# A decoder layer in split fp32r: the order of the twelve products of a half step

## The chip, the cores and the metric

The kernel runs on one core of one Trainium2 chip. The metric is the device time of one execution in microseconds (us); a lower time is better. Three runs of the kernel before gave a median of 2371.65 us (2369.32 to 2371.7).

## The reference, cut to what matters

One decoder layer is computed for 256 tokens of 2048 channels, in fp32. Two gated feed-forward nets lie around a mixer that adds a retention branch and a windowed attention branch:

```python
x = x + 0.5 * mod[:, 2] * swiglu(modulate(rms_norm(x, norm_ffn1)), w_ffn1_gu, w_ffn1_down)
h = modulate(rms_norm(x, norm_mix))
x = x + mod[:, 5] * token_mixing(h, w_in, w_ret_branch, w_swa_branch, w_out, sinks)
x = x + 0.5 * mod[:, 8] * swiglu(modulate(rms_norm(x, norm_ffn2)), w_ffn2_gu, w_ffn2_down)
return rms_norm(x, norm_final)
```

Nearly all of the arithmetic is in products of the 256 token rows with big fp32 weights (2048 x 11264, 5632 x 2048, 2048 x 13312 and three of 2048 x 2048). `mod` comes from a condition vector `c` and a weight of 2048 x 18432, as sums over products rather than as a matrix product on the tensor engine.

## The kernel before, in words

**Splitting.** A number is split into a high part (rounded to fp32r) and a low part (the difference), and a product of two numbers is made of three: high by high, low activation by high weight, and high activation by low weight. `split` (L365 to L373) makes the two parts of a weight tile: ScalarE casts `wh` (L369), VectorE subtracts `wl` (L371). Activations are split the same way, either once into a held pair (`Held`, tiles `hh` and `hl`) or when they are used (`Whole.pair`, cast L404 and subtraction L405, tile `a`).

**Tiling.** A weight block is 512 of the contracted channels by 512 columns (1 MB, one DMA, `load`, L346, four buffers `raw`). A half of it, 256 channels by 512 columns, is one half step: one call of `split` and one call of `products`. The 256 tokens are two tiles of 128 (t = 0 and 1), each with a PSUM bank of its own that accumulates over the half steps. `wh` and `wl` have three buffers each (pool `wsp`), and the accumulating banks four (`acc`). A half step has two blocks of 128 channels (j), two token tiles (t) and three products, so twelve matmuls of 128 x 128 by 128 x 512. The stationary operand is a 128 x 128 piece of the activation, the moving one a 128 x 512 piece of the weight.

**Order in `products` (L349 to L363).** The loops run over j, then over t, and inside that come the three products of one j and one t: L356 high by high, L357 low activation, L359 low weight. All three add into the same bank. The last matmul is put into the list `newest`, which other code uses to place its own matmuls behind it (`issue_after(newest[-1])`).

**Who sets the order on the engines.** For most of the kernel the order of the program is a priority only: a scheduler with a timeline model goes through the instructions, and each engine is given the first one in program order whose inputs are ready in that model. So what an engine runs can differ from the program's order. Only the sync engine's queue (the weight loads) is always in written order. In the stages marked `manual_schedule(engines=ORDERED)`, which are the start and the ends of the three down products, PE, DVE and ACT too run in written order. There `last` calls `products` for one t at a time, and a written list (`ORDER`) interleaves the parts of it with a norm.

**What else uses the engines.** `gemm` and `gemm_part` walk the half steps; after each `products` call `tick` adds some passes of the conditioning sums (VectorE, L219). The softmax of the windowed attention and the retention run beside the input projection (between about 860 and 1210 us of the span). Results leave the banks through VectorE or ScalarE (L637, L702, L1158 and others).

Of the kernel before, what the change touches and what calls it, by code (L numbers as in the profile page):

```python
# [17 lines left out]
P = 128  # L18
# [59 lines left out]
def layer_kernel(  # L78
# [22 lines left out]
    nc = tc.nc  # L101
# [246 lines left out]

    def products(banks, ah, al, wh, wl, starts, ends, halves=range(NT)):  # L349
        n = ah.shape[1]  # L350
        for j in range(n):
            first, last = starts and j == 0, ends and j == n - 1
            for t in halves:
                ts = slice(t * P, (t + 1) * P)
                ps = banks[t]
                nc.tensor.matmul(ps, ah[:, j, ts], wh[:, j, :], start=first, stop=False)  # L356
                nc.tensor.matmul(ps, al[:, j, ts], wh[:, j, :], start=False, stop=False)  # L357
                newest.append(
                    nc.tensor.matmul(  # L359
                        ps, ah[:, j, ts], wl[:, j, :], start=False, stop=last  # L360
                    ).ins
                )
                del newest[:-1]  # L363

    def split(pool, tag, src, n, hi_engine="act"):  # L365
        k = src.shape[1]
# [8 lines left out]
    cast, low, newest = [], [], []  # L375
# [48 lines left out]
    def gemm_part(act, w, col0s, banks, kb, KT, ahead=None, close=None):  # L424

        pairs = [act.pair(kb * 2 + h) for h in range(2)]
        for i, c0 in enumerate(col0s):
            raw = None if ahead else load(w, kb, c0)
            for h in range(2):
                if ahead:  # L430
                    wh, wl = ahead[h]
                else:
                    wh, wl = split(wsp, "w", raw[:, 2 * h : 2 * h + 2, :], CH)
                ah, al = pairs[h]
                ends = kb * KB + 2 * h + 2 == KT or (i == close and h == 1)
                products(banks[i], ah, al, wh, wl, kb + h == 0, ends)
                tick()
            turn_step()

    def gemm(act, w, col0s, KT=KD, ahead=None):  # L440
        banks = [[acc_bank() for _ in range(NT)] for _ in col0s]
        for kb in range(KT // KB):
            gemm_part(act, w, col0s, banks, kb, KT, None if kb else ahead)
            step()
        return banks
# [285 lines left out]
    def down_product(act, w, gate, KT, spare, before, after, parted=False):  # L731
# [16 lines left out]
        with tc.manual_schedule(engines=ORDERED):  # L748
# [16 lines left out]
            for kb in (a - 2, a - 1, a, b):  # L765
                wt = weight(w, kb, c0s[0])
                pairs[kb] = []
                for h in range(2):
                    pairs[kb].append(act.pair(kb * 2 + h, place(kb, h)))
                    products(  # L770
                        banks[0], *pairs[kb][h], *wt(h), kb + h == 0, kb == b and h == 1
                    )
                n = {a - 2: a - 2, a - 1: a, a: b, b: a - 1}[kb]
                wt = weight(
                    w, n, c0s[1], spare if n == a - 2 else None if n < a else home_views()
                )
                late[n] = [(n, h, wt(h)) for h in range(2)]
            steps = [step for kb in (a - 2, a, a - 1, b) for step in late[kb]]

            def last(t, which, to=None, cs=slice(0, CH)):  # L780
                to = banks[1] if to is None else to
                for kb, h, (wh, wl) in which:
                    starts = kb == a - 2 and h == 0 if parted else kb + h == 0
                    products(
                        to, *pairs[kb][h], wh[:, :, cs], wl[:, :, cs],
                        starts, kb == b and h == 1, [t],
                    )
# [260 lines left out]
    banks, moved = {}, set()  # L1048
# [118 lines left out]
    for g, ks in enumerate(groups):  # L1167
# [7 lines left out]
        for i, n in enumerate(order):  # L1175
# [5 lines left out]
            last = len(order) - 2  # L1181
# [94 lines left out]
    halves = [slice(i * HD, (i + 1) * HD) for i in range(2)]  # L1276
# [227 lines left out]
    def gates(p):  # L1504

        sg = slot().rearrange("p (g i t n) -> p g i t n", g=2, i=2, t=NT)
        for g, off in ((0, O_GR), (1, O_GS)):
            for i in range(2):
                b = in_chunk(off + (2 * p + i) * CH)
                for t in range(NT):  # L1510
                    nc.scalar.activation(sg[:, g, i, t, :], b[t], AF.Sigmoid)
        return sg

    first = gates(0)
# [17 lines left out]
    for p in range(2):  # L1532
        sg = first if p == 0 else gates(p)
        c0s = [(2 * p + i) * CH for i in range(2)]
        for g, a, w in ((1, a_swa, w_swa_branch), (0, a_ret, w_ret_branch)):
            assert g == 1 or not turns
            banks = gemm(a, w[0], c0s)
# [149 lines left out]
```

## Time and profile before

| what | value |
|---|---|
| three runs, median | 2371.65 us (2369.32 to 2371.7) |
| profiled execution, first to last instruction (span) | 2366.2 us |
| PE (matmul) busy | 2343.0 us, 99% |
| PEld (weight load) busy | 1920.2 us, 81% |
| DVE busy | 1703.8 us, 72% |
| ACT busy | 1312.3 us, 55% |
| HBM | 254 GB/s over the span |

The profile gives no time for the profiled execution other than its span, which is 5.45 us below the median of the runs. PE is the matmul queue, PEld the loads of the stationary operand, DVE the vector engine, ACT the scalar engine, SP the engine that issues the weight loads. "L359" is line 359 of the kernel. A row "out<-in" names the tile written and the tiles read. Idle time stands before an instruction, with the engine or DMA that ended it. A matmul's recorded end is modelled, and records of consecutive matmuls overlap, so the distance between two starts is what shows the rate.

### The profile page before, as it was taken

What the parts mean: (1) busy time and instruction counts of PE and PEld (TensorE: products, weight loads), DVE (VectorE), ACT (ScalarE), POOL (GpSimd) and SP (SyncE); (2) the same over time, 40 slices, a digit from 0 to 9 for tenths busy, and PEclk for the clock granted to TensorE, in tenths of its full rate; (3) what the DMA queues carried; (4) which work ended last, traced back from release to release, by engine and by line L of the source; (5) the groups of instructions that cost most, each with busy time, mean ns of one, the idle gap of its engine ahead of it and who ended that gap; (6) DMA issues with size and microseconds to landing.
All of it is one profiled execution on the core that took longest, in us unless ns stands there. A gap on an engine that the chain in (4) does not pass through costs nothing.

```text
span 2366.2 us, 28355 instructions
## 1 busy us (share of the span) xinstructions
PE 2343.0 (99%) x10479; PEld 1920.2 (81%) x10479; DVE 1703.8 (72%) x2628; ACT 1312.3 (55%) x1780; POOL 9.2 (0%) x21
## 2 busy tenths in 40 slices
PE   8999999999999999999999999999999999999998
PEld 5888888888788887778888888888888888888887
DVE  7887799778877768976777776677555555555656
ACT  6544456455546568775556564466455455455544
POOL 0000000000000000000000000000000000000000
PEclk9999999999999999999999999999999999999999
DMA  9977789998866889876778787764777777666553
GB/s 385 362 289 268 273 294 356 347 346 334 315 251 231 282 274 238 252 222 244 271 275 292 300 297 282 289 208 179 246 237 257 247 240 262 239 214 203 193 196 125
DMA packets 186316, 627.87 MB, mean 265 GB/s; under 512 B 108801, under 2 KB 109185, under 8 KB 115649
## 3 DMA queue, kind: packets, MB, share of 16 engines
q1 hardware_dynamic: 183682, 615.05, 74.8%
q0 software_dynamic: 1600, 9.83, 1.0%
q8 instruction: 82, 1.34, 0.2%
q10 hardware_dynamic: 896, 1.19, 0.1%
q14 instruction: 56, 0.46, 0.1%
HBM read 597.16 MB, written 4.22 MB: 254 GB/s over the span
## 4 chain that ended last, share of the span: by engine, by line
PE 55%; DVE 1%; issue 0%; ACT 0%; DVEq 0%
PE pa L359 18%; PE pa L356 18%; PE pa L357 18%; DVE wl L371 0%; PE ps L1372 0%; PE pd L1457 0%; PE pd L1471 0%; PE pd L1470 0%; PE pd L1472 0%; PE ps L888 0%; DVE spare L480 0%; DVE soft L1359 0%; PE ps L359 0%; PE ps L357 0%; PE ps L356 0%
## 5 line engine op out<-in xcount | busy, mean ns | idle before, releaser
L369 ACT CAST wh<-raw 128x1024 fp32r<-128x1024 f32 x792 | 831.7, 1053 | 915.3 <-PE pa L357 881.4
L371 DVE TENSOR_TENSOR wl<-raw,wh 128x1024 fp32r<-128x1024 f32 x792 | 961.3, 1222 | 519.4 <-ACT wh L369 516.3
L356 PE MATMUL pa<-wh,hh 128*128 128x512 f32 x2184 | 854.0, 391 | 1.7 <-ACT wh L369 1.7
L357 PE MATMUL pa<-wh,hl 128*128 128x512 f32 x2184 | 850.4, 389 | 0.0
L359 PE MATMUL pa<-wl,hh 128*128 128x512 f32 x2184 | 773.3, 391 | 1.9 <-DVE wl L371 1.8
L356 PEld LDWEIGHTS pa<-wh,hh 128*128 128x128 f32 x2184 | 409.9, 188 | 90.3 <-ACT wh L369 2.8
L359 PEld LDWEIGHTS pa<-wl,hh 128*128 128x128 f32 x2184 | 408.3, 188 | 91.1 <-DVE wl L371 5.5
L357 PEld LDWEIGHTS pa<-wh,hl 128*128 128x128 f32 x2184 | 410.1, 188 | 84.7 <-issue 0.2
L357 PE MATMUL pa<-wh,a 128*128 128x512 f32 x912 | 353.4, 389 | 0.3 <-DVE a L405 0.3
L356 PE MATMUL pa<-wh,a 128*128 128x512 f32 x912 | 337.6, 389 | 1.8 <-DVE t L637 1.8
L359 PE MATMUL pa<-wl,a 128*128 128x512 f32 x912 | 335.8, 389 | 0.4 <-DVE wl L371 0.4
L219 DVE CUSTOM_DVE_ANT_0 slot<-slot,cact 128x512 f32<-128x512 f32 (+2 forms) x272 | 209.4, 819 | 12.8 <-DMA slot<-in_w_ada_dram 12.7
L356 PEld LDWEIGHTS pa<-wh,a 128*128 128x128 f32 x912 | 171.0, 188 | 37.7 <-DVE t L637 2.2
L357 PEld LDWEIGHTS pa<-wh,a 128*128 128x128 f32 x912 | 171.1, 188 | 37.2 <-DVE a L405 1.9
L359 PEld LDWEIGHTS pa<-wl,a 128*128 128x128 f32 x912 | 171.1, 188 | 36.1 <-DVE wl L371 0.8
L545 ACT COPY slot<-back 128x512 uint16<-128x512 uint16 x140 | 93.3, 765 | 0.0
L219 DVE CUSTOM_DVE_ANT_0 rows_x<-rows_x,cact 128x512 f32<-128x512 f32 x124 | 78.7, 687 | 11.3 <-DMA rows_x<-in_w_ada_dram 10.9
L219 DVE CUSTOM_DVE_ANT_0 raw<-raw,cact 128x512 f32<-128x512 f32 (+1 forms) x108 | 70.8, 706 | 18.3 <-DMA raw<-in_w_ada_dram 18.0
L405 DVE TENSOR_TENSOR a<-slot,a 128x512 fp32r<-128x512 f32 x114 | 77.8, 684 | 0.3 <-ACT a L404 0.3
L529 ACT COPY flat<-t 128x512 uint16<-128x512 uint16 x128 | 72.7, 617 | 3.0 <-DVE t L1445 2.5
L404 ACT CAST a<-slot 128x512 fp32r<-128x512 f32 x114 | 70.3, 618 | 0.1
L219 DVE DVE_READ_ACCUMULATOR2_ANT sums<- 128x1 f32 x504 | 41.1, 82 | 0.0
(252 smaller groups left out, 1246.7 us busy)
## 6 DMA issues: line engine op xcount, KB each, us to landing
raw<-in_w_ffn_gu_dram SPq DMA_DIRECT2D x160, 1024.0 KB, 5.1
raw<-in_w_in_dram SPq DMA_DIRECT2D x104, 1024.0 KB, 5.8
raw<-in_w_ffn_down_dram SPq DMA_DIRECT2D x88, 1024.0 KB, 4.9
slot<-in_w_ada_dram SPq DMA_DIRECT2D x83, 1024.0 KB, 7.0
rows_x<-in_w_ada_dram SPq DMA_DIRECT2D x31, 1024.0 KB, 7.1
raw<-in_w_ada_dram SPq DMA_DIRECT2D x26, 1024.0 KB, 5.7
raw<-in_w_swa_branch_dram SPq DMA_DIRECT2D x16, 1024.0 KB, 6.4
raw<-in_w_ret_branch_dram SPq DMA_DIRECT2D x16, 1024.0 KB, 5.5
```

Of the source, the lines that this page charges most:

```text
L219: nc.vector.tensor_tensor_reduce(out=w[:, at], in0=w[:, at], in1=cact[:, at], scale=1.0, scalar=0.0, op0=ALU.mult, op1=ALU.add, accum_out= ...
L356: nc.tensor.matmul(ps, ah[:, j, ts], wh[:, j, :], start=first, stop=False)
L357: nc.tensor.matmul(ps, al[:, j, ts], wh[:, j, :], start=False, stop=False)
L359: nc.tensor.matmul(ps, ah[:, j, ts], wl[:, j, :], start=False, stop=last).ins
L369: cast.append(nc.scalar.copy(hi, src).ins)
L371: low.append(nc.vector.tensor_sub(lo, src, hi.bitcast(F32)).ins)
L404: nc.scalar.copy(hi, v)
L405: nc.vector.tensor_sub(lo, v, hi.bitcast(F32))
L529: nc.scalar.copy(planes[:, i, :], words(src)[:, :, i])
L545: nc.scalar.copy(into[:, :, :, i], held["turned"][:, i])
```

## The change

The three products become the outer loop. First come the four high by high products of the half step (j = 0 with both t, j = 1 with both t), then the four with the activation's low part, then the four with the weight's low part. The number of matmuls, their operands and their sizes are the same. The first matmul of the first row starts the accumulation of its bank, and the last row ends it. `newest` holds the last matmul of the call.

```diff
     def products(banks, ah, al, wh, wl, starts, ends, halves=range(NT)):
         n = ah.shape[1]
-        for j in range(n):
-            first, last = starts and j == 0, ends and j == n - 1
-            for t in halves:
-                ts = slice(t * P, (t + 1) * P)
-                ps = banks[t]
-                nc.tensor.matmul(ps, ah[:, j, ts], wh[:, j, :], start=first, stop=False)
-                nc.tensor.matmul(ps, al[:, j, ts], wh[:, j, :], start=False, stop=False)
-                newest.append(
-                    nc.tensor.matmul(
-                        ps, ah[:, j, ts], wl[:, j, :], start=False, stop=last
-                    ).ins
-                )
-                del newest[:-1]
+        parts = ((ah, wh), (al, wh), (ah, wl))
+        for i, (act, weights) in enumerate(parts):
+            for j in range(n):
+                for t in halves:
+                    product = nc.tensor.matmul(
+                        banks[t],
+                        act[:, j, t * P : (t + 1) * P],
+                        weights[:, j, :],
+                        start=starts and i == 0 and j == 0,
+                        stop=ends and i == 2 and j == n - 1,
+                    )
+        newest.append(product.ins)
+        del newest[:-1]
```

## Prediction, written before the change was run

> **What bounds the kernel now.** I read the page first: which engine fills the span, and the costliest groups.
>
> ```profile
> span 2366.2 us, 28355 instructions
> PE 2343.0 (99%) x10479; PEld 1920.2 (81%) x10479; DVE 1703.8 (72%) x2628; ACT 1312.3 (55%) x1780; POOL 9.2 (0%) x21
> ...
> L369 ACT CAST wh<-raw 128x1024 fp32r<-128x1024 f32 x792 | 831.7, 1053 | 915.3 <-PE pa L357 881.4
> L371 DVE TENSOR_TENSOR wl<-raw,wh 128x1024 fp32r<-128x1024 f32 x792 | 961.3, 1222 | 519.4 <-ACT wh L369 516.3
> L356 PE MATMUL pa<-wh,hh 128*128 128x512 f32 x2184 | 854.0, 391 | 1.7 <-ACT wh L369 1.7
> L357 PE MATMUL pa<-wh,hl 128*128 128x512 f32 x2184 | 850.4, 389 | 0.0
> L359 PE MATMUL pa<-wl,hh 128*128 128x512 f32 x2184 | 773.3, 391 | 1.9 <-DVE wl L371 1.8
> ...
> L357 PE MATMUL pa<-wh,a 128*128 128x512 f32 x912 | 353.4, 389 | 0.3 <-DVE a L405 0.3
> ```
>
> PE fills 99% of the span. Each of the three lines runs 2184 + 912 = 3096 times in the two big groups alone, so 9288 products, or 774 half steps of twelve. The last columns say how little PE waits. ScalarE, by contrast, sat idle for 881.4 us because it waited for the last product that reads an old `wh`: the splits are made ahead, as far as the three buffers allow.
>
> Second, the busy time by window, for the rate of a stretch with nothing but products, and the granted clock by core:
>
> ```profile
> 1800.00:1900.00 100.00, 100.00 (x443) 82.81 (x442) 57.69 (x76) 49.76 (x57) 0.00 (x0) 1.00 0.72 244
> core 0: 2366.2 us, clock 0.999
> ```
>
> The first count is that of PE: 100 us hold about 441 whole products (443 touch the window), so 0.227 us each; the clock is fully granted. Nothing in the change alters this rate unless the order itself does, which the timeline of PE can show, since the scheduler already strays from the written order:
>
> ```profile
> 1700.19 0.39 PE L357 MATMUL pa<-wh,hl 128*128 128x512 f32 x1
> 1700.41 0.39 PE L356 MATMUL pa<-wh,hh 128*128 128x512 f32 x1
> 1700.64 0.39 PE L357 MATMUL pa<-wh,hl 128*128 128x512 f32 x1
> 1700.87 0.62 PE L359 MATMUL pa<-wl,hh 128*128 128x512 f32 x2
> 1701.32 0.39 PE L356 MATMUL pa<-wh,hh 128*128 128x512 f32 x1
> ```
>
> Here the two token tiles' high and low-activation products run first and the two low-weight products follow as a pair: in this group the first low-weight product is already the fifth of its half step, not the third. The pair takes 0.62 us, which is 0.39 + 0.23, and the next starts 0.45 us after the pair began: two products on two banks, with the same moving tile, at 0.225 us each. Steps within one bank (L356 to L357) take 0.22 to 0.23 us too. So the order as such is free in this trace.
>
> That leaves the waits of the two PE queues, third:
>
> ```profile
> PE pa L359 <- DVE wl L371: 2.5, 6, 0.9
> PE pa L356 <- DVE t L637: 1.8, 1, 1.8
> PE pa L356 <- ACT wh L369: 1.7, 2, 1.2
> PE pa L357 <- DVE a L405: 0.3, 1, 0.3
> ...
> PEld pa L359 <- DVE wl L371: 7.6, 15, 1.3
> PEld pa L357 <- DVE a L405: 1.9, 4, 0.7
> ```
>
> The waits for a low part of a weight (`wl`) and of an activation (`a`) are all that the new order can relieve directly. The rest of the span that isn't products is the start, the small matmuls of softmax and retention and the norm at the end, which the change leaves alone.
>
> **What a wait costs.** The columns are total us, times, longest. A PE row counts only idle time behind a matmul's modelled end, 0.39 us after its start, whereas the next could start after 0.227; so 0.16 us of each wait is missing. The timeline around some of the waits shows this and a second loss:
>
> ```profile
> 862.97 0.39 PE L357 MATMUL pa<-wh,hl 128*128 128x512 f32 x1
> 863.87 0.73 PE L359 MATMUL pa<-wl,hh 128*128 128x512 f32 x2 [0.51 <-DVE wl L371]
> ...
> 42.90 0.39 PE L357 MATMUL pa<-wh,hl 128*128 128x512 f32 x1
> 43.48 0.73 PE L359 MATMUL pa<-wl,hh 128*128 128x512 f32 x2 [0.19 <-DVE wl L371]
> ...
> 48.15 0.50 PE L356 MATMUL pa<-wh,hh 128*128 128x512 f32 x1 [1.20 <-ACT wh L369]
> ...
> 62.20 0.39 PE L357 MATMUL pa<-wh,hl 128*128 128x512 f32 x1
> 62.76 0.73 PE L359 MATMUL pa<-wl,hh 128*128 128x512 f32 x2 [0.18 <-DVE wl L371]
> ...
> 1042.93 0.39 PE L359 MATMUL pa<-wl,hh 128*128 128x512 f32 x1
> 1044.24 0.74 PE L359 MATMUL pa<-wl,hh 128*128 128x512 f32 x2 [0.92 <-DVE wl L371]
> ```
>
> At 863.87 the start is 0.90 us after the one before it, so 0.67 late; and the pair behind it takes 0.73 instead of 0.62, so 0.11 more, 0.78 in all for an idle time of 0.51. So each wait in a PE row costs its idle time and 0.16 + 0.11 = 0.27 more; a wait that shows only in the load queue is hidden under the modelled end and costs between 0 and 0.27.
>
> **The change part by part.**
>
> Nothing is removed or added: same matmuls, same loads, same DMAs, and SP's and POOL's queues are not passed by anything. Four things move.
>
> First, the low weight's first use. In the written order it is third, in the scheduled one often fifth; it becomes ninth, so 4 to 6 products or 0.91 to 1.36 us later. What the six and the nine hidden `wl` waits cost now: 2.5 + 6 x 0.27 = 4.1 us, and 0 to 9 x 0.27 = 2.4 more, so 4.1 to 6.5.
>
> Second, the low activation's first use goes from second or third to fifth, 0.45 to 0.68 us later. What those waits cost now: 0.3 + 0.27 = 0.57, and 0 to 3 x 0.27 = 0.8 more, so 0.6 to 1.4. Together 4.7 to 7.9; I take the middle, 6.3 us, as what both sorts of wait cost now.
>
> Third, `wh` is read last by the eighth product instead of the eleventh, so its buffer is free 0.68 us earlier. The cast (1.05 us) and the subtraction (1.22 us) behind it begin that much sooner, though the subtraction still needs the buffer of `wl`, which comes free with the twelfth as before. The cast alone takes 4.6 products, so it ends about when the twelfth does: nothing new waits there. This adds up to 0.68 us of slack for each split and could relieve the two `wh` waits (1.7 + 2 x 0.27 = 2.2 us); I count none of it, since the wait at 48.15 stands in a crowded stretch, and keep 2.2 for the range.
>
> Fourth, the second token tile's bank is needed by the second product instead of the fourth, 0.45 us sooner. That matters only where a bank is just being emptied. There is one such wait in the trace, for L637 (1.8 us), and I leave it as it is; the cost is 0 to 0.45.
>
> What of the 6.3 goes? The new slack of 0.91 us or more covers a delay of 0.67 at 863.87 or 0.35 at 43.48. It does not cover all of 1044.24: that start is 1.31 us after the one before, so 1.08 late, and 0.17 with its 0.11 would stay: 0.3 is kept. In the first 70 us a removed wait is likely to be found again: the two quoted there cost 0.46 and 0.44 (0.35 + 0.11 and 0.33 + 0.11), and at 48.15 PE waits 1.2 us for a cast, which a PE that comes earlier only waits longer for. Of these 0.9 I keep half, 0.45. Lastly, the scheduler draws up a new plan with the new order, and the new plan will have late tiles of its own. No row shows how many. The bounds are: none, or as many as now (6.3 over 19 waits, and the gain gone). With more slack everywhere I take three of the mean size 0.33, about 0.9 us. Sum: -6.3 + 0.3 + 0.45 + 0.9 = -4.65.
>
> So the profiled execution's 2366.2 us would become 2361.5. That span is 5.45 us under the median of the runs, and I take the same difference from the median: 2371.65 - 4.65 = 2367.0 us, 0.196% less. About 0.2%, or 4.7 us, is what a measurement of this kernel can tell from no change; the forecast lies on that line.
>
> **The rivals.**
>
> *The waits go somewhere else (no change that can be measured).* ScalarE and VectorE then bound those stretches and not the order: the 1.2 us wait for a cast five us behind 43.48 speaks for it, against it stands that DVE is 72% busy and that its splits wait for PE most of the time. If half of the 6.3 comes back, as waits for `wh` or in the new plan, 3.2 us are left: 2368.5.
>
> *Every wait goes (clearly faster).* All 7.9 of the upper bound and the 2.2 of the `wh` waits: 10.1 us, so 2361.6. Against it: the crowded start.
>
> *A change of bank at each product costs time (slower).* Before, the written order changes bank four times in twelve products, after it twelve times; 774 half steps make 8 x 774 = 6192 more changes. At p ns each that is 6.2 x p us. It cancels the gain at 0.75 ns, and at 1.5 ns the kernel is slower by 9.3 - 4.65 = 4.65, at 2376.3. Against it speaks the pair at 1700.87, which changes bank at an unaltered rate, within the rows' hundredths. For it: those rows show only two products in a row that change bank, so a long alternation is not shown.
> [...]
>
> *The new plan is worse (slower).* The softmax and retention stretch has its small matmuls placed behind the newest product; a plan that puts bursts on DVE before the splits would bring more waits like that at 1044.24 (1.08 + 0.11 = 1.2 us). Four of them (4.8 us) use up the forecast gain, and from there it is slower; eight of them, 9.6 us, give 2376.6. Against it: every split has slack added and none removed.
>
> That the change doesn't do what it says is possible in part: the scheduler already runs part of the low-weight products late, so for those half steps the new order is nearer to the old one than the diff looks. This is in the sum through the fifth place.
>
> **How the numbers follow.** My forecast with all waits but a few gone: 0.44 for a gain around 4 to 6 us. Half of it given back: 0.33. Every wait gone: 0.10. Bank changes: 0.05. A worse plan: 0.08. Of the forecast, which lies on the line, three quarters count as faster (0.33), with the 0.10 of the third case 0.43; the rest and the half-gain case are within 0.2%, 0.11 + 0.33 = 0.44; the two slow cases make 0.05 + 0.08 = 0.13. The likeliest time is 2367.0. The range takes in the every-wait-gone case (2361.6, and 1 us for the scatter of the runs below it) and most of the two slower cases (2376.3 and 2376.6): 2360.5 to 2376.5.
>
> **What would show it.** In the changed profile the timeline of PE should read four high, four low-activation and four low-weight products, 0.227 us apart. The waits of PE and its load queue for `wl` should fall from 2.5 and 7.6 us to under 1 and 3, those for `a` to near 0. ScalarE's wait for PE should name the low-activation product as before and stay near 881 us. A window of products only should still hold about 443. I am wrong if that count falls by one or more in a hundred us (banks or clock), if the granted clock falls below 0.995, or if waits for `wh` grow by what those for `wl` lose.

## The result, and the profile after

| | before | after |
|---|---|---|
| median of five runs | 2371.55 us (2369.32 to 2371.7) | 2360.42 us (2359.91 to 2361.44) |
| span of the profiled execution | 2366.2 us | 2359.1 us |

The ratio is 0.996 (95% interval 0.9949 to 0.9971): the new order is faster by 0.3 to 0.5%, 11.1 us between the medians. The forecast was 2367.0, so the direction was right and the gain was more than twice the 4.65 us of the sum; the time lies 0.08 us below the stated range. The kernel before had lower medians in the groups of runs further down, 2368.89 to 2369.87 us over 23 to 27 runs each. Against those the gain would be 8.5 to 9.5 us, but the kernel after was not run in those groups, so 11.1 us, from five runs of each, may be somewhat too much. One run of a kernel further down, the new order with three raw blocks, took 4809 us for a reason that is not known; that kernel's median is 2368.01 us with this run and 2367.72 without it.

The page of the kernel after, its span, its engines, and the groups that answer to those of before (all products stand on line 355 now):

```profile
span 2359.1 us, 28364 instructions
PE 2338.8 (99%) x10479; PEld 1921.2 (81%) x10479; DVE 1697.5 (72%) x2628; ACT 1314.8 (56%) x1779; POOL 9.2 (0%) x21
...
L369 ACT CAST wh<-raw 128x1024 fp32r<-128x1024 f32 x792 | 831.1, 1054 | 883.3 <-PE pa L355 836.7
L371 DVE TENSOR_TENSOR wl<-raw,wh 128x1024 fp32r<-128x1024 f32 x792 | 960.8, 1222 | 478.0 <-ACT wh L369 416.6
L355 PE MATMUL pa<-wh,hh 128*128 128x512 f32 x2184 | 595.5, 392 | 2.2 <-ACT wh L369 1.6
L355 PE MATMUL pa<-wh,hl 128*128 128x512 f32 x2184 | 589.7, 389 | 0.0
L355 PE MATMUL pa<-wl,hh 128*128 128x512 f32 x2184 | 585.2, 390 | 0.4 <-DVE wl L371 0.3
```

The work is the same, instruction for instruction on PE. What fell is idle time before the `wl` products (1.9 to 0.4 us here) and the time for which DVE waited for a cast (516.3 to 416.6 us). The busy us of the PE rows can't be compared with before, since overlapping records of one line are counted once.

The timeline of PE and a window of products only, kernel after:

```profile
1699.74 1.07 PE L355 MATMUL pa<-wh,hh 128*128 128x512 f32 x4
1700.64 1.07 PE L355 MATMUL pa<-wh,hl 128*128 128x512 f32 x4
1701.55 1.07 PE L355 MATMUL pa<-wl,hh 128*128 128x512 f32 x4
1702.46 1.07 PE L355 MATMUL pa<-wh,hh 128*128 128x512 f32 x4
```

```profile
1800.00:1900.00 100.00, 100.00 (x443) 82.81 (x442) 56.96 (x74) 52.46 (x63) 0.00 (x0) 1.00 0.72 237
```

Four of each sort, 0.907 us from row to row, 0.227 each, and 443 matmuls in the window as before. So a change of bank at every product costs nothing that this window shows; its clock reads 1.00 (third from the end), as in the same window of before.

The waits of PE and of its load queue in the kernel after:

```profile
PE pa L355 <- ACT wh L369: 1.6, 3, 1.0
PE pa L355 <- DVE slot L1540: 0.6, 1, 0.6
PE pa L355 <- DVE wl L371: 0.3, 1, 0.3
...
PEld pa L355 <- ACT wh L369: 4.2, 6, 1.4
PEld pa L355 <- DVE wl L371: 1.3, 2, 0.7
PEld pa L355 <- DVE a L405: 0.4, 1, 0.4
```

Waits for `wl` fell from 6 and 15 to 1 and 2, those for `a` from 1 and 4 to 0 and 1. The wait for a bank (L637, 1.8 us) is gone as well; one of 0.6 us for another bank (L1540) is new. Most signs came as forecast. One did not: ScalarE's wait for PE was to stay near 881 us, and it fell to 836.7 (the row of L369 above). That row belongs to the third step of the prediction, the earlier release of the high weight, to which its sum gave nothing. The next question is where 11.1 us can come from when the waits that I could find came to 6.3.

### The profile page after: what moved, and what is told of

Same layout as the page of the kernel before. It is cut to its first block, busy times and chain, and to the rows that moved or that the text cites. A ratio compares the mean times of both kernels' runs of the same rounds, so it can differ in the third digit from the quotient of the medians.

```text
span 2359.1 us, 28364 instructions
## 1 busy us (share of the span) xinstructions
PE 2338.8 (99%) x10479; PEld 1921.2 (81%) x10479; DVE 1697.5 (72%) x2628; ACT 1314.8 (56%) x1779; POOL 9.2 (0%) x21
## 4 chain that ended last, share of the span: by engine, by line
PE 97%; DMA 1%; DVE 1%; ACT 0%; issue 0%; SPq 0%; DVEq 0%; ACTq 0%
PE pa L355 95%; PE ps L1372 0%; DMA slot<-in_w_ada_dram 0%; DMA rows_x<-in_w_ada_dram 0%; PE pd L1288 0%; DVE slot L219 0%; DMA x_sb<-in_x_dram 0%; PE ps L355 0%; PE ps L888 0%; DVE wl L371 0%; PE ps L512 0%; ACT wh L369 0%; DVE rows_x L219 0%; PE ps L1288 0%; PE pd L1470 0%
## 5 line engine op out<-in xcount | busy, mean ns | idle before, releaser
L369 ACT CAST wh<-raw 128x1024 fp32r<-128x1024 f32 x792 | 831.1, 1054 | 883.3 <-PE pa L355 836.7
L371 DVE TENSOR_TENSOR wl<-raw,wh 128x1024 fp32r<-128x1024 f32 x792 | 960.8, 1222 | 478.0 <-ACT wh L369 416.6
L355 PE MATMUL pa<-wh,hh 128*128 128x512 f32 x2184 | 595.5, 392 | 2.2 <-ACT wh L369 1.6
L355 PE MATMUL pa<-wh,hl 128*128 128x512 f32 x2184 | 589.7, 389 | 0.0
L355 PE MATMUL pa<-wl,hh 128*128 128x512 f32 x2184 | 585.2, 390 | 0.4 <-DVE wl L371 0.3
L355 PE MATMUL pa<-wh,a 128*128 128x512 f32 x1824 | 452.4, 389 | 0.0
L355 PE MATMUL pa<-wl,a 128*128 128x512 f32 x912 | 245.2, 389 | 0.0
L1155 DVE TENSOR_TENSOR slot<-slot,pa 128x512 f32<-128x512 f32 x48 | 31.0, 683 | 16.7 <-PE pa L355 16.7
L355 PE MATMUL pa<-wh,home 128*128 128x512 f32 x160 | 39.5, 389 | 0.0
```

The costliest lines, as they stand in the source:

```text
L355: product = nc.tensor.matmul(banks[t], act[:, j, t * P : (t + 1) * P], weights[:, j, :], start=starts and i == 0 and j == 0, stop=ends and ...
L369: cast.append(nc.scalar.copy(hi, src).ins)
L371: low.append(nc.vector.tensor_sub(lo, src, hi.bitcast(F32)).ins)
L1155: nc.vector.tensor_add(p, p, b)
```

## The experiments

The twelve kernels were run in three groups of four, each group on one chip together with runs of the kernel before. A kernel is compared with the median of before in its own group: 2368.89 us for the first four, 2369.63 for the next four, 2369.87 for the last four.

**The kernel before, profiled again.** No edit.

> The kernel before, unchanged, profiled once more. The first profile had a span of 2366.2 us while the runs had a median of 2371.55; the kernel after has 2359.1 and 2360.42, so the gap between the two kernels is 7.1 us by span and 11.1 us by run time. If the first profile of before caught a short execution, this span is about 2369 to 2370 (2371.5 less the 1.8 us that lie outside the span in the run of after) and shows more or longer waits. If the 5.4 us really lie outside the span in this kernel, this span is 2366 again. Ratio to before 1.000.

Measured: 2370.78 us, ratio 1.0004 (0.9995 to 1.0013); the span of this profile is 2370.6. The first part came true, a little above the 2369 to 2370 us expected. In every run 1.7 to 1.9 us lie outside the span, for both kernels, so the first profile of before was an execution of about 2368.0 us, shorter than all five runs beside it. This one, 2372.4 us, is a long one: the spans of the 23 runs of before in this group reach from 2365.0 to 2371.1 us. The waits of the long execution:

```profile
PE pa L359 <- DVE wl L371: 4.5, 8, 1.4
PE pa L356 <- DVE t L637: 1.8, 1, 1.8
PE pa L356 <- ACT wh L369: 1.7, 2, 1.2
...
PEld pa L359 <- DVE wl L371: 11.3, 18, 1.8
```

Waits for `wl` are 11.3 us instead of 7.6 in the load queue. Comparing the starts of the matmuls tells where. The table holds the start of the n-th matmul of the trace, in us from the start of the span, in the kernel after less that in the two executions of before (in the two orders the n-th matmul need not be the same product):

| matmul no. | its start, short execution of before | after less short execution | after less long execution |
|---|---|---|---|
| 200 | 68 us | -0.49 | -0.46 |
| 1400 | 337 us | -0.42 | -0.41 |
| 2000 | 471 us | -0.56 | -4.58 |
| 2300 | 539 us | -0.92 | -4.95 |
| 2800 | 656 us | -4.28 | -9.24 |
| 4600 | 1045 us | -7.19 | -11.26 |
| 6100 | 1379 us | -5.71 | -9.98 |
| last | 2358 us | -7.15 | -11.54 |

The 4 us between 337 and 471 us are there in one execution and not in the other. The timeline of DVE in the long one shows one of their sources:

```profile
464.92 2.36 DVE L371 TENSOR_TENSOR wl<-raw,wh 128x1024 fp32r<-128x1024 f32 x2 [5.62 <-ACT wh L369]
469.56 0.69 DVE L219 CUSTOM_DVE_ANT_0 slot<-slot,cact 128x512 f32<-128x512 f32 x1 [2.27 <-DMA slot<-in_w_ada_dram]
...
472.01 2.36 DVE L371 TENSOR_TENSOR wl<-raw,wh 128x1024 fp32r<-128x1024 f32 x2
```

A conditioning pass waits 2.27 us for its row, and the next two subtractions stand behind it until 472.01; PE then starts a `wl` product 1.74 us after the one before it, at 473.29. In the short execution the pass ahead of the same subtraction did not wait for its row. So how late a row lands differs from one execution to the next, and the old order pays a sum that varies. In the stretch from 640 us, where the wait for the bank stands, a second thing differs. PE in the long execution:

```profile
641.63 0.50 PE L356 MATMUL pa<-wh,a 128*128 128x512 f32 x1 [1.77 <-DVE t L637]
641.97 0.40 PE L357 MATMUL pa<-wh,a 128*128 128x512 f32 x1
642.76 1.22 PE L359 MATMUL pa<-wl,a 128*128 128x512 f32 x2 [0.40 <-DVE wl L371]
643.78 0.63 PE L356 MATMUL pa<-wh,a 128*128 128x512 f32 x1
644.21 0.63 PE L357 MATMUL pa<-wh,a 128*128 128x512 f32 x1
644.63 0.63 PE L359 MATMUL pa<-wl,a 128*128 128x512 f32 x1
...
646.94 0.39 PE L359 MATMUL pa<-wl,a 128*128 128x512 f32 x1
```

```profile
643.40:646.00 2.60, 2.60 (x8) 2.02 (x7) 2.60 (x4) 0.98 (x3) 0.00 (x0) 0.50 0.03 6
646.00:649.00 3.00, 3.00 (x15) 2.46 (x13) 3.00 (x9) 1.96 (x5) 0.00 (x0) 0.98 0.98 350
```

After the same two waits that the short execution had, six products come 0.427 us apart instead of 0.227, and the clock column (third from the end) reads 0.50. That is 1.2 us more for the wait. I had priced a wait at its idle time and 0.27.

**The order taken apart.** Four kernels change only `products`, from the new order. The first keeps the rows and goes bank by bank inside a row:

```diff
-            for j in range(n):
-                for t in halves:
+            for t in halves:
+                for j in range(n):
```

> Rows as in the changed kernel, but inside a row both products of one bank come first and then both of the other, so there are six changes of bank in a half step instead of twelve. Theory of slack (low parts needed later): as the changed kernel, 2360.4, within 1 us. Rival, the bank changes cost time: at p ns each there are some 5000 fewer, so 5 us less per ns; faster than the changed kernel by over 1 us would speak for it. A window of products alone should hold 443 matmuls in 100 us either way by the first theory.

Measured: 2362.71 us, ratio 0.9973 (0.9962 to 0.9984). That is 6.2 us under before, with half of the bank changes. It is not faster than the new order, so the rival of the bank changes falls; it is 2.3 us slower, where 1 us was expected at most, for a reason that was not looked for.

The second puts the low weight's row in the middle:

```diff
-        parts = ((ah, wh), (al, wh), (ah, wl))
+        parts = ((ah, wh), (ah, wl), (al, wh))
```

> Rows in the order high, low weight, low activation: the low weight is first needed by the fifth product, where the scheduled order of before mostly had it, the high weight is read last by the twelfth product (before: eleventh, changed: eighth), and the low activation is first needed by the ninth. Theory of slack for the low weight: most of its waits come back, about 4 to 5 us, so 2365 to 2366 if the second down-product half keeps its 3.4 us and 2369 if not. Rival, the gain is in how the banks are closed (both banks' last products are neighbours, so the vector engine's plan empties both before it turns to other work): nothing but that matters, so 2361 to 2362. Rival, the earlier release of the high weight is what counts: worse than before, above 2371.

Measured: 2369.70 us, ratio 1.0007 (0.9998 to 1.0016). Nothing is left of the gain, though the wait for the bank at L637 is gone in this kernel too. So how the banks are closed is not the cause. The low weight is needed early again here, but the high weight is also held to the end, so two theories are still alive.

The third keeps high and low activation together and moves only the low-weight products:

```diff
...
+        turns = [(p, j, t) for j in range(n) for t in halves for p in (high, low_a)]
+        turns += [(low_w, j, t) for j in range(n) for t in halves]
...
```

> High and low activation stay neighbours as in before, for each block and bank, and only the four low-weight products are moved to the end; so the low weight is first needed by the ninth product, the low activation by the second, and the high weight is read last by the eighth. Theory of slack for the low weight: keeps all but the waits for low activations (four of them, about 1.2 us), so 2361 to 2362. If the rows as a whole (bank changes at each product, low activation later) were what counted, it would be nearer to before: 2365 or more.

Measured: 2360.95 us, ratio 0.9965 (0.9952 to 0.9977). That is 7.9 us under before, and within 0.6 us of the time of the new order, without rows and with the low activation still needed second. Here too the low weight is late and the high weight is free early.

**Late need or early release.** The two are told apart by the next pair. One needs the low weight late and holds the high weight to the last product:

```diff
...
+        turns = rows[0] + rows[1][:-1] + rows[2] + rows[1][-1:]
...
```

> Order of a half step: four high, three low activation, four low weight, and the last low-activation product at the very end. The low weight is first needed by the eighth product (changed kernel: ninth, before: mostly fifth), but the high weight is read last by the twelfth (changed: eighth, before: eleventh). Theory that the later need of the low weight is the cause: near the changed kernel, 6 to 8 us under before. Theory that both count as slack in the same coin (products between the release of one buffer and the need of its next content: 29 before, 36 changed, 31 here): a third of the gain, 2 to 3 us under before. Theory that the early release of the high weight is the cause: as before, or 1 us worse.

Measured: 2370.67 us, ratio 1.0006 (0.9997 to 1.0015). The other needs the low weight at the fifth product and frees the high weight after the ninth:

```diff
...
+        for j in range(n):
+            rows = [[(p, j, t) for t in halves] for p in (high, low_a, low_w)]
+            turns += rows[0] + rows[1] + (rows[2][:1] if j < n - 1 else left + rows[2])
+            left = rows[2][1:]
...
```

> The mirror of the run with the held high weight. Order: two high, two low activation and one low weight for the first block, then two high and two low activation of the second, then the other three low weight. The low weight is first needed by the fifth product as in the scheduled order of before, and the high weight is read last by the ninth. Theory that the later need of the low weight is the cause: as before, within 1 us. Slack in the same coin (31 products here as well): 2 to 3 us under before. Early release as the cause: near the changed kernel, 5 us or more under before.

Measured: 2362.54 us, ratio 0.9968 (0.9955 to 0.998), 7.1 us under before. This is the opposite of what I had reasoned: the gain goes with the early release, and the kernel with the late need alone shows none. Slack in one coin falls too, since both kernels have 31 products of it. The mirror is not perfect: the scheduler ran the first low-weight product of the second kernel fifth in 399 of its 800 half steps and seventh in 220, against fifth in 514 in before. The waits of the two, the held high weight first:

```profile
PE pa L356 <- ACT wh L370: 4.4, 6, 2.1
PE pa L356 <- DVE a L406: 1.3, 2, 1.0
PE pa L356 <- DVE wl L372: 0.8, 3, 0.4
```

```profile
PE pa L358 <- ACT wh L372: 1.8, 3, 0.8
PE pa L358 <- DVE wl L374: 0.5, 1, 0.5
```

A late need does take away the waits for `wl` (2.5 in before, 0.8 here). But the casts begin later, and PE waits for `wh` instead: 4.4 us against 1.7. With the early release both are small. The worst of the new waits, in PE's timeline and clock of the kernel with the held high weight:

```profile
984.51 0.39 PE L356 MATMUL pa<-wh,hl 128*128 128x512 f32 x1
987.04 1.80 PE L356 MATMUL pa<-wh,hh 128*128 128x512 f32 x4 [2.14 <-ACT wh L370]
```

```profile
986.50:991.00 4.50, 3.96 (x10) 3.12 (x11) 4.48 (x5) 4.50 (x7) 0.00 (x0) 0.62 1.05 342
```

2.5 us between two starts, and a mean clock of 0.62 over the 4.50 us from 986.50 us. If the rest of that stretch had the full clock, 3.4 us of it were at 0.50, or eight products of 0.427 us, by an estimate from this row. The three products from 988.63 us on are 0.427 us apart. ScalarE just before:

```profile
982.34 0.40 ACT L1318 ACTIVATE soft<-soft,ng 128x128 f32<-128x128 f32 x1 [4.38 <-DVE ng L1312]
...
985.96 2.92 ACT L370 CAST wh<-raw 128x1024 fp32r<-128x1024 f32 x3
```

The buffer of this cast had come free at about 977.8 us, when the last product that reads its old content ended. ScalarE ended the cast before it at 977.95 us, but then waited 4.38 us for the softmax, which stands ahead of this cast in its queue. So the wait comes from the place that the plan gave the cast, and one such place weighs much: 2.30 us late, 0.11 behind it and eight products 0.2 us longer are 4.0 us, by an estimate from these rows. Without it the kernel would lie about 3 us under before, by the same estimate. So the late need may be worth something; that it is worth nothing is not shown. By this estimate it is still worth less than the early release.

How far ahead the splits run can be worked out from these traces: the time from the end of a cast or a subtraction to the start of the first product that reads it, over 800 pairs.

| kernel | `wh` free after product | cast ahead, median us | `wl` ready under 0.3 us ahead |
|---|---|---|---|
| before, short / long execution | 11 | 4.41 / 4.41 | 16 / 19 |
| after | 8 | 5.09 | 2 |
| rows by bank | 8 | 5.09 | 6 |
| low weight last | 8 | 5.09 | 3 |
| early weight, free high | 9 | 4.87 | 7 |
| low weight second | 12 | 4.18 | 20 |
| late weight, held high | 12 | 4.18 | 9 |

The casts follow the release product by product: three products earlier is 0.68 us more lead. In before and after, 610 and 623 of 797 casts begin within 0.2 us of the end of the last product that reads their buffer.

**Conditioning rows earlier.** In the kernel before:

```diff
-            set_pace(ROWS_FFN1, 32 * 192 // 32, place_row, 1)
+            set_pace(ROWS_FFN1, 32 * 192 // 32, place_row, AQ)
```

> The kernel before with one edit: in the rest of the first feed-forward net the conditioning rows are loaded four passes ahead instead of one. In the long execution of before, PE lost 4.0 us more between 340 and 480 us than in the short one, each time for a low weight that stood behind a conditioning pass that waited for its row. If that is the source of the variable part, those waits shrink here, the runs scatter less and the median is 2 to 4 us under before. If the rows are late however early they are asked for (they share the queue with the weights), it is as before or slower, since they also hold weight buffers for longer.

Measured: 2369.01 us, ratio 0.9992 (0.9983 to 1.0001). This decides nothing: the median moves by 0.6 us, within the interval, the runs scatter as much as before (2366.26 to 2372.03), and its one profile (span 2367.5) shows a wait for `wl` of 2.4 us at 639 us in place of that for the bank. That late rows are a source of the variable part is seen in the trace of the long execution; that asking for them earlier would help is not shown.

**The new order only where a bank closes.** `products` of before, with the rows under `if ends:`.

> The new order only in the half steps that close a bank, the old order in all others. Theory that the wait for a bank at the second half of the first down product (1.9 us of late start before, none after) goes because both token tiles of a bank pair close one product apart instead of three, so that the plan empties both before it turns to conditioning passes: that wait goes, 1.9 us under before or a little more, and the waits for low weights stay as they were. If that wait went only because the whole plan moved, it stays: as before.

Measured: 2372.98 us, ratio 1.0015 (1.0006 to 1.0024). The wait at L637 is gone from its profile, and yet it is slower: PE starts 2.07 us late at 465 us for a `wh`, and the mean clock of the profiled execution is 0.998, as with the held high weight; the first profile of before has 0.999. The expected 1.9 us went, and others came. So one wait taken away by a new plan says little of the sum.

**The same by a buffer.** If the early release is what counts, a fourth buffer for the high weights must do as much in the old order, and must add little to the new. Room for it is made by three raw blocks instead of four, and all four kernels have three:

```diff
-RAWS = 4
+RAWS = 3
...
+    whp = ctx.enter_context(tc.tile_pool(name="whp", bufs=4))
...
-        hi = pool.tile([P, 2, n], F32R, tag=tag + "h", name=nm(tag + "h"))[:, :k, :]
+        hi = whp.tile([P, 2, n], F32R, tag=tag + "h", name=nm(tag + "h"))[:, :k, :]
...
```

The two kernels with three high buffers have the same pool with `bufs=3`.

> Control for the run with a fourth buffer: the kernel before with three instead of four buffers for raw weight blocks (8 KB per partition less) and the high weights in a pool of their own, still with three buffers. It can only be slower than before; how much is not the question, 0 to 15 us.

> The old order of products with a fourth buffer for the high weights (three raw blocks make room). The cast of a high weight need no longer wait for the product that last reads a buffer a half step later: the wait that the new order shortens by three products is shortened by twelve, and the low weight is needed as early as before. Theory that the earlier release of the high weight is the cause: 5 us or more under the control with three. Theory that the later need of the low weight is the cause, or that any new plan is as good: within 2 us of that control.

> The new order (rows) with three raw blocks and three buffers for the high weights. By any theory of slack 7 to 11 us under the control with the old order, as with four raw blocks. If three raw blocks make the loads the bound, the difference shrinks.

> The new order with three raw blocks and four buffers for the high weights. If the new order acts by the earlier release, the fourth buffer has nothing left to give: within 2 us of the run of rows with three. If it acts by the later need of the low weight, the two add up, and it is faster than both.

Measured, with the ratio to the unchanged kernel before (2369.87 us in this group):

| | three high buffers | four high buffers |
|---|---|---|
| old order | 2382.29 us, 1.0052 (1.0038 to 1.0065) | 2368.41 us, 0.9994 (0.9985 to 1.0003) |
| new order | 2368.01 us, 0.9992 (0.9983 to 1.0001) | 2366.28 us, 0.9986 (0.9977 to 0.9995) |

The fourth buffer takes 13.9 us off the old order, the new order 14.3, and both together 16.0. The first was expected to be 5 us or more, the second 7 to 11. Each does most of what the other does: the second adds 1.7 to 2.1 us. The waits of the two old-order kernels, three buffers first:

```profile
PE pa L358 <- DVE a L406: 4.6, 3, 2.3
PE pa L357 <- ACT wh L370: 4.0, 5, 1.2
PE pa L360 <- DVE wl L372: 3.1, 7, 0.6
```

```profile
PE pa L358 <- DVE a L406: 3.0, 2, 1.7
PE pa L357 <- ACT wh L370: 2.5, 2, 1.3
PE pa L360 <- DVE wl L372: 0.8, 3, 0.3
```

All three sorts shrink, those for `wl` most, although the low weight is needed no later: with four buffers its first product is the third in 340 of the 800 half steps and the fifth in 219, with three the fifth in 513. The casts have a median lead of 7.1 us with four and 4.41 with three. In the profiles the clock differs too: 0.998 with three buffers, where two starts that wait for `a` are 2.38 and 2.44 us late (527.55 and 1303.27 us), and 0.999 with four, where the two that answer to them are 1.42 and 1.88 us late. That the clock is part of the 13.9 us is not shown: three of the five runs with three buffers have 0.999 and take 2381.01 to 2383.42 us. Three raw blocks cost 12.4 us by themselves, so these sizes hold for a kernel that is shorter of buffers; that the two remedies replace each other is what carries over. None of these beats the new order with four raw blocks.

## Why the prediction was right in direction and wrong in size

**What bounds the kernel** held: PE, at 0.227 us a product in both orders (443 products touch the window of 100 us in each), with a few waits beside it.

**The third step failed.** "Third, `wh` is read last by the eighth product instead of the eleventh ... I count none of it." This is the part that the gain goes with. The four orders that free `wh` after the eighth or ninth product are all faster than before, by 6.2 to 11.1 us; with `wh` held to the twelfth product the gain is gone; and a spare buffer gives the same. I had given the whole of the gain to the first step, the later need of the low weight. That step does cut waits for `wl`, but the one kernel that had it alone was no faster. So the direction came out right in part by luck. Why 0.68 us of lead goes so far is argued from the traces and tested by no run: a cast that starts later delays the subtraction that reads it, and each can then come to stand behind other work of its engine, as in the traces above the two subtractions behind a conditioning pass that waited 2.27 us for its row, and the cast behind the exponentials of a softmax that waited 4.38 us. Whether the earlier release works on the chip itself, or through the plan that the scheduler draws up from it, was not separated; every kernel here has a plan of its own, and the wait at 987 us shows how much a plan can do.

**The offset failed.** "I take the same difference from the median", 5.45 us, took a short execution for a typical one. 1.78 us lie outside the span, and the old order loses 4 us more in a long execution, while the five runs of the new order lie within 1.6 us. By the two profiles the gain is 7.1 or 11.5 us; the five runs say 11.1, the medians of before in the later groups 8.5 to 9.5. I had no second execution, but 5.45 us outside the span should have made me ask.

**The price of a wait** was too low for the longest. Idle time and 0.27 us holds at 863.87, but not at 642 us of the long execution, where the clock behind the wait was 0.50 and six products took 1.2 us more.

**The fourth step failed**: "I leave it as it is". With the waits for low parts around it, the stretch at the bank wait gave 3.4 us (from 539 to 656 us in the table) or 4.3.

**The terms taken off.** 0.45 us for the first 70 us was too little: by 68 us 0.49 us is won, of which 0.44 is there at 30 us already, ahead of the waits in question, so next to nothing came there. For new waits I took 0.9 us; the profile has 1.4: 0.75 late with 0.08 behind it at L1540 (1365.62 us), and 0.49 with 0.11 for a `wl` at 1147.33.

**The rivals.** "Every wait goes", 2361.6 us, came nearest in time, but by luck, with waits that were not in my list. The change of bank costs nothing that the windows show (443 products before and after, and 443 with the rows by bank). The clock did not fall with it either: all five runs of the kernel after have 0.999, as has the first profile of before. The worse plan is real, but in other kernels: the rows at closing half steps alone are slower by 0.15%.

## What to carry to other kernels

Where a buffer limits how far ahead an operand is prepared, order its readers so that the last one comes early: here that was worth as much as one more buffer, in a kernel with three raw blocks. Price a wait on the engine that bounds the kernel by what follows as well (here 1.2 us more behind the waits at 642 us), and look at the clock in the microseconds behind it. One profile of a kernel whose runs scatter is one draw: compare its span with the runs before summing its waits.

## What the runs showed of the hardware

In the traces of this case a few late starts of PE have a stretch of lower clock behind them. Two are printed above. With the held high weight the clock is 0.62 over the 4.50 us that hold a start 2.30 us late (987.04 us), and three products behind it come 0.427 us apart instead of 0.227. In the long execution of before, starts 1.93 and 0.57 us late (641.63 and 642.76 us) have a clock of 0.50 behind them from 643.40 to 646.00 us, with products 0.427 us apart; from there to 649.00 us it is 0.98. The short execution has starts 1.92 and 0.57 us late (637.60 and 638.73 us), and its clock is 1.00 all the same from 637 to 649 us. So the traces give no length of wait from which on the clock falls.

Over whole executions, the clock of a profile goes with the longest late start past the first 30 us. Besides the held high weight, four of the 14 profiles have starts over 2 us late: the rows at closing half steps (2.07, at 465 us), the early conditioning rows (2.60, at 639 us), the new order with three raw blocks (2.16, at 1608 us) and the old order with three raw blocks (2.38 and 2.44), the last two with three high buffers. The mean clock of these five, and of the long execution of before, is 0.998. In the other eight no start is more than 1.92 us late, and it is 0.999. In the kernel after, the longest wait between products makes a start 1.13 us late (52.83 us), with a clock of 1.00 from 50 to 57 us.

The time of a run goes with its clock in the same sense. In the first group, 10 of the 23 runs of the kernel before had a mean clock of 0.998 and took 2370.5 us on average, and 13 had 0.999 and took 2368.7. In the other two groups the difference has the same sign but is smaller: 2370.3 against 2369.2 us, and 2370.2 against 2369.9.
